# A two-layer RG-LRU / attention block: the attention pieces' time plan shifted, the last gate's vectors moved into the attention, row transposes spread over the first head

## The chip, the cores and the metric

The kernel runs on one core of a Trainium2 chip. The metric is the device time of one execution in microseconds (us). The engines are named as the profile names them: PE (TensorE, matmuls and transposes, with PEld for its weight loads), DVE (VectorE), ACT (ScalarE), POOL (GpSimd) and SP (SyncE, which issues most of the loads here).

## The reference

Two layers run over 512 latent and 256 context tokens of width 2048, all in float32. Layer 0 is a bidirectional RG-LRU, layer 1 a differential attention with 16 heads of two 64-wide parts. Each layer is a norm modulated by a condition vector c, a mixer, and a residual gated by a vector of its own that also comes from c (a product of silu(c) with a 2048-wide matrix, "the gate").

```
for i in range(DEPTH):                       # i = 0 RG-LRU, i = 1 attention
    shift, scale, gate = split(silu(c) @ mod_w[i] + mod_b[i], 3)
    h = rms_norm(x, norm_g[i]) * (1 + scale) + shift     # context too, with c_ctx
    x = x + gate * mixer_i(h, h_ctx)
# attention, per head; q, k normed and rotated; keys are 512 + 256 tokens
    p0, p1 = softmax(q0 @ k0.T), softmax(q1 @ k1.T)
    o = (p0 - lam * p1) @ v
    y = rms_norm(o, subln_g) * (1 - lam_init) * silu(g)   # then y @ w_out
```

## The kernel before

Every float32 product is made of three matmuls on split operands: a weight tile `raw` (128x1024, 512 KB) is cast to its high half `wh` by ACT (line 54), DVE subtracts to get the low half `wl` (line 57), and a step is h times wh, h times wl, low h times wh. Two `raw` buffers take the loads of all weights in turn. PE's order is the order in which the code is written; the other engines and SP's queue are ordered by the compiler's scheduler, and then run strictly in that order.

The program has four stages. The first makes the modulation and the RG-LRU (to about 720 us of the trace). `phase2` is its out-projection: four column blocks n of 512, each 16 steps of six token tiles, with six PSUM accumulators `acc` (lines 530 to 532); `evac` scales by the gate row, adds to x, and sums squares. Beside it runs `mod_stream`, the products of the gates: a 512 KB tile `mw` of the transposed matrix is loaded, and DVE multiplies it by silu(c), broadcast over the partitions, and sums each row (line 108, 128x1024). The gates of layer 0 need both c and c_ctx, so two products a tile; layer 1's gate needs one (32 tiles, the blocks 48 to 63 in two halves). After the last block come the norm of the rows and `norm1`: for each of 16 column tiles kt, the tokens' rows are transposed by PE (`tps`, line 234: four tiles of a latent group or two of the context's) and `h_evac` makes h and its low half, in ACT and DVE. The latent group's 16 turns run before the context tiles' last block is done, the context group's inside head 0.

`phase3` is the attention, `head` by `head`. Head hd's projection has 96 steps, written (b, t, k): four blocks b of weights (two raw tiles each), six token tiles t (t 4 and 5 half as wide), four column tiles k. A step of full width is three matmuls `pj` (lines 676 to 678). Between these steps stand the pieces of the attention of the head before, at due times on a planner's clock that adds 0.68 (0.36 for t 4 and 5) a step and COST a piece; `merged` puts a piece ahead of the first step at which the clock has come to its due time, and what is left behind the last step. These due times are the table PLAN. The pieces:

- k0, k1, q: k and q by channels, transposed.
- s00 to s31: scores of query tile 0 to 3, softmax part 0 or 1, in the one PSUM buffer `sc` (line 754). DVE takes the maximum (756), ACT the exponential with its sum (761), DVE joins the two parts.
- t0a to t3b: transposes of a query tile's probabilities, first four key tiles, then two (`atr`, line 779), into the one PSUM buffer `tr`; ACT casts, DVE subtracts (`athl`).
- v0, v1: their product with v for two query tiles (`o`, lines 790 to 792, 18 matmuls); ACT copies it out.
- o0, o1: transposes of the output back (`otr`, line 802); ACT copies it (804) and squares it.
- f (line 811): DVE's rsqrt of the output's norm (815, 816, and lines 81 to 83) and four products with the gate path (820). y: the transposes of the result (`otr`, line 827).

A prime marks a piece of the head before that one: o1', f' and y' stand early in the next head, since v1 ends the table. At the same place the next head's `qk_norm` runs on DVE: squares' sums (`qv`, 704), rotary products (`pr`, `rt`, 714 to 717) and the scaling (719).

The last turn (hd 16) has no projection; its steps are those of the attention's out-projection (`out_chunks`, two blocks of 64), its own o1, f and y have due times in LAST, and head 15's share of the first block comes at the end.

Of the kernel before, what the change touches and what calls it, by code (L numbers as in the profile page):

```python
# [32 lines left out]
PLAN = ((0.3, "o1'"), (0.5, "f'"), (5.0, "y'"), (17.0, "k0"), (20.5, "k1"), (24.0, "q"), (27.5, "s00"), (31.5, "s01"), (35.5, "s10"),  # L33
        (37.0, "t0a"), (39.2, "t0b"), (39.6, "s11"), (43.6, "s20"), (45.2, "t1a"), (47.4, "t1b"), (47.6, "s21"), (49.6, "v0"),
        (51.8, "s30"), (53.2, "o0"), (54.0, "t2a"), (56.2, "t2b"), (56.4, "s31"), (61.6, "t3a"), (63.8, "t3b"), (66.0, "v1"))
LAST = ((69.5, "o1"), (70.0, "f"), (74.5, "y"))
COST = {"o": 0.2, "f": 0.0, "y": 0.2, "k": 0.3, "q": 0.4, "s": 0.7, "t": 0.3, "v": 2.2}
# [6 lines left out]
class Kern:  # L44
# [114 lines left out]
    def run(self):  # L159
# [379 lines left out]
    def phase2(self):  # L539
# [5 lines left out]
        with tc.tile_pool(name="p2", bufs=1, reuse_waits="tile") as pool:  # L545
            col = pool.tile([128, 64, 2, 2], F32, tag="mcl", name="mcl")
            chunk = lambda h, n, end: [(h, b, 2, end) for b in range(32 + 4 * n, 36 + 4 * n)]
            gates = self.mod_stream(pool, col, chunk(0, 1, 0) + chunk(1, 1, 1) + chunk(1, 2, 0) + chunk(0, 2, 1) + chunk(0, 3, 0)
                                    + chunk(1, 3, 1) + [(h, b, 1, 1 - h) for h in (1, 0) for b in range(48, 64)])
            xt = []  # L550
            for i in range(NTOK):
                t = (pool if i < 4 else pb).tile([128, D], F32, tag=f"x{i}", name=f"x1_{i}")
                xt.append(t)
            ss = [pb.tile([128, GROUPS[g][1], 4], F32, tag=f"ss{g}", name=f"ss{g}") for g in range(2)]
            norm = iter(())
            for n in range(4):
                gt = pool.tile([128, 2, 512], F32, tag="gt", name="gt")
                for grp in ((range(6),) if n < 3 else (range(4), range(4, 6))):
                    acc = {t: self.psum("acc") for t in grp}
# [11 lines left out]
                    for b in range(4):  # L571
                        w = []
                        for u in (2 * b, 2 * b + 1):
                            w.append(self.weights(a["w_out"][n, u], (2, 512)))
                            for _ in range(2 if n > 1 or u % 2 else 1):
                                next(gates, None)
# [8 lines left out]
                        for t in grp:  # L585
                            for k in range(4):
                                self.out_mm(acc, w[k // 2], k % 2, 4 * b + k, (t,))
                            if b:
                                for _ in range(3):
                                    next(norm, None)  # L590
                            if b == 3:
                                evac(t)
                    for _ in norm:
                        pass
                    if n == 3:
# [13 lines left out]
                        norm = self.norm1(g, xt, pb)  # L609
        return norm, lambda: poolb.__exit__(None, None, None)  # L610

    def norm1(self, g, xt, pool):
        for kt in range(KT):
            self.norm_group(1, g, (kt,), xt, pool)
# [44 lines left out]
    def load(self, pool, name, shape, src):  # L659
# [3 lines left out]
        return t  # L663

# [237 lines left out]
    def phase3(self, rest, done):  # L902
# [4 lines left out]
        self.p3a = self.ctx3.enter_context(tc.tile_pool(name="p3c", bufs=1, reuse_waits="tile"))  # L907
        prev = None
        with tc.manual_schedule(engines={nc.tensor.engine}):
            for hd in range(HEADS + 1):  # L910
                prev = self.head(hd, prev, rest, done)
        self.ctx3.close()

    def head(self, hd, prev, rest, done):
# [39 lines left out]
        if last:  # L954
# [130 lines left out]
```

## Time and profile before

| | |
|---|---|
| Time of a run | 2526.28 us median of 3 runs (2524.82 to 2530.53) |
| The profiled execution | 2525.51 us; its span in the trace 2523.7 us |
| Granted TensorE clock, mean | 0.97 of full speed |
| PE busy | 93% of the span |
| DVE busy | 63% |
| ACT busy | 45% |
| DMA, 119 GB/s on average | the queue that carries the weights takes 33.7% of 16 engines' span |

The span is what the trace holds, the time also holds what lies around it. A busy share is an average over the four stages; PE's busy time is that of pipelined matmuls, whose starts are 0.23 us apart while each is shown with 0.39. A granted clock of 1.00 is 2.4 GHz, 0.50 is 1.2 GHz.

### The profile page before, as it was taken

To read this page: it belongs to the slowest core of one execution; us is meant where nothing else is said; L and a number is where in the kernel's file an instruction comes from. 1 tells how busy PE (TensorE), PEld (TensorE's weight loads), DVE (VectorE), ACT (ScalarE), POOL (GpSimd) and SP (SyncE) were. 2 spreads that over 40 slices of the span, in tenths; PEclk is the share of its full clock that TensorE was granted. 3 is DMA by queue.
4 is the path that set the end of the run, shared out by engine and by line. 5 is a ranking of instruction groups with operands and counts; after the bars stand their busy time and mean duration, and the time that the engine had idled before them with its cause. 6 is when DMAs were issued, how large, how long until landed. Compare 5 with 4: busy or idle time off the path is not lost.

```text
span 2523.7 us, 32331 instructions
## 1 busy us (share of the span) xinstructions
PE 2335.4 (93%) x12529; PEld 1943.8 (77%) x12544; DVE 1592.4 (63%) x3029; ACT 1124.0 (45%) x1965; POOL 9.2 (0%) x20
## 2 busy tenths in 40 slices
PE   5989999999999999798999989998999989988999
PEld 4678888888888777587877777777877777777787
DVE  4459999999567756446555564555555564556643
ACT  5367656756862114544433343333433344344421
POOL 0001000000000000000000000000000000000000
PEclk9999999999999999899999999999999999999999
DMA  9915554543247776121121111111121111123242
GB/s 359 377 60 171 179 179 157 172 156 133 73 145 260 254 254 216 52 84 55 52 70 55 55 51 55 55 55 55 59 63 55 55 52 53 55 94 108 80 159 75
DMA packets 93448, 299.43 MB, mean 119 GB/s; under 512 B 11696, under 2 KB 16112, under 8 KB 93296
## 3 DMA queue, kind: packets, MB, share of 16 engines
q1 hardware_dynamic: 88544, 288.41, 33.7%
q10 hardware_dynamic: 4752, 8.98, 0.9%
q8 instruction: 98, 1.61, 0.3%
q14 instruction: 54, 0.44, 0.1%
HBM read 278.52 MB, written 18.83 MB: 118 GB/s over the span
## 4 chain that ended last, share of the span: by engine, by line
PE 54%; DVE 18%; ACT 9%; DMA 7%; issue 4%; SPq 0%; POOL 0%; ACTq 0%; DVEq 0%
PE pj L676 9%; PE pj L677 9%; PE pj L678 9%; DVE wl L57 4%; DMA mw<-mod_t 4%; PE proj L340 4%; PE proj L338 4%; PE proj L342 4%; PE sc L754 3%; ACT wh L54 2%; DVE mw L108 2%; PE acc L532 2%; PE acc L530 2%; PE acc L531 2%; ACT p L761 2%
## 5 line engine op out<-in xcount | busy, mean ns | idle before, releaser
L676 PE MATMUL pj<-wh,h 128*128 128x512 f32 (+1 forms) x1536 | 575.2, 375 | 9.1 <-DVE tmp L564 9.1
L677 PE MATMUL pj<-wl,h 128*128 128x512 f32 (+1 forms) x1536 | 557.0, 363 | 0.1
L678 PE MATMUL pj<-wh,h 128*128 128x512 f32 (+1 forms) x1536 | 555.2, 361 | 0.0
L57 DVE TENSOR_TENSOR wl<-raw,wh 128x1024 fp32r<-128x1024 f32 x264 | 319.0, 1220 | 244.0 <-ACT wh L54 240.8
L54 ACT CAST wh<-raw 128x1024 fp32r<-128x1024 f32 x264 | 271.8, 1050 | 447.3 <-PE pj L678 127.2
L676 PEld LDWEIGHTS pj<-wh,h 128*128 128x128 f32 x1536 | 299.3, 195 | 44.6 <-DVE tmp L564 9.5
L678 PEld LDWEIGHTS pj<-wh,h 128*128 128x128 f32 x1536 | 296.3, 193 | 44.8
L677 PEld LDWEIGHTS pj<-wl,h 128*128 128x128 f32 x1536 | 297.9, 194 | 35.9 <-DVE wl L57 1.0
L338 PE MATMUL proj<-h,wh 128*128 128x256 f32 (+1 forms) x1024 | 270.0, 342 | 7.3 <-DVE h L56 6.2
L340 PE MATMUL proj<-h,wh 128*128 128x512 f32 (+1 forms) x1024 | 276.0, 341 | 0.0
L342 PE MATMUL proj<-h,wl 128*128 128x512 f32 (+1 forms) x1024 | 275.0, 340 | 0.0
L338 PEld LDWEIGHTS proj<-h,wh 128*128 128x128 f32 x1024 | 161.2, 189 | 37.3 <-DVE h L56 7.2
L761 ACT ACTIVATE p<-sc,mx 128x768 f32<-128x768 f32 x128 | 116.2, 908 | 165.1 <-DVE mx L756 164.7
L342 PEld LDWEIGHTS proj<-h,wl 128*128 128x128 f32 x1024 | 162.6, 189 | 25.4 <-issue 2.1
L340 PEld LDWEIGHTS proj<-h,wh 128*128 128x128 f32 x1024 | 162.5, 189 | 25.5 <-issue 2.5
L108 DVE SCALAR_TENSOR_TENSOR mw<-mw,sb 128x1024 f32<-128x1024 f32 x128 | 155.7, 1217 | 39.7 <-DMA mw<-mod_t 32.3
L531 PE MATMUL acc<-wl,h 128*128 128x512 f32 x384 | 154.0, 401 | 12.8 <-DVE wl L57 12.8
L756 DVE TENSOR_REDUCE mx<-sc 128x1 f32<-128x768 f32 x128 | 122.1, 954 | 58.3 <-PE sc L754 57.7
L530 PE MATMUL acc<-wh,h 128*128 128x512 f32 x384 | 153.0, 398 | 1.9 <-ACT wh L54 1.9
L532 PE MATMUL acc<-wh,h 128*128 128x512 f32 x384 | 152.6, 397 | 0.0
L108 DVE SCALAR_TENSOR_TENSOR mj<-mw,sb 128x1024 bf16<-128x1024 f32 x96 | 116.8, 1217 | 36.5 <-DMA mw<-mod_t 18.6
L57 DVE TENSOR_TENSOR athl<-atr,athl 128x512 fp32r<-128x512 f32 (+1 forms) x128 | 71.1, 555 | 91.0 <-ACT athl L54 91.0
(237 smaller groups left out, 3461.2 us busy)
## 6 DMA issues: line engine op xcount, KB each, us to landing
mw<-mod_t SPq DMA_DIRECT2D x128, 512.0 KB, 3.4
raw<-w_att SPq DMA_DIRECT2D x128, 512.0 KB, 3.2
mw<-mod_w SPq DMA_DIRECT2D x64, 512.0 KB, 10.2
raw<-w_in SPq DMA_DIRECT2D x64, 512.0 KB, 3.4
raw<-w_out SPq DMA_DIRECT2D x40, 512.0 KB, 4.5
raw<-w_o SPq DMA_DIRECT2D x32, 512.0 KB, 3.5
sb<-crow SPq DMA_DIRECT2D x7, 1024.0 KB, 6.4
yd<-sg SPq DMA_DIRECT2D x15, 384.0 KB, 3.5
```

The costliest lines, as they stand in the source:

```text
L54: nc.scalar.copy(hi, raw)
L57: return lo_eng.tensor_tensor(lo, raw, hi.bitcast(F32), op=ALU.subtract)
L108: nc.vector.scalar_tensor_tensor(o, w, 1.0, self.sb[:, m, :], op0=ALU.mult, op1=ALU.mult, accum_out=col[:, blk, h, m:m + 1])
L338: nc.tensor.matmul(ps[g][:, :GW[g]], wh, h[g][:, 0, :], start=first, stop=False)
L340: nc.tensor.matmul(ps[g][:, :GW[g]], wh, h[g][:, 1, :], start=False, stop=False)
L342: nc.tensor.matmul(ps[g][:, :GW[g]], wl, h[g][:, 0, :], start=False, stop=last)
L530: nc.tensor.matmul(acc[t], yh, wh, start=(kt == first), stop=False)
L531: nc.tensor.matmul(acc[t], yh, wl, start=False, stop=False)
L532: nc.tensor.matmul(acc[t], yl, wh, start=False, stop=(kt == last))
L676: nc.tensor.matmul(o, h[:, 0, c], wh, start=(kt == 0 and t < 4), stop=False)
L677: nc.tensor.matmul(o, h[:, 0, c], wl, start=False, stop=False)
L678: nc.tensor.matmul(o, h[:, 1, c], wh, start=False, stop=(kt == KT - 1 and t != 4))
```

## The change

The table PLAN gets other due times (all pieces keep their kind; t2b and s31 trade places). In LAST the gate rows of the last out-projection become pieces (g0, g1), and head 15's share of the first block (z) too. The products of layer 1's gate leave `phase2`: a new function `gate1_stream` loads the same 32 tiles of 512 KB into the `raw` buffers, as steps that `fillers` sets at t 3 of the blocks b 0 to 2 in heads 1 to 11, each with two products of half the width. `mod_stream` now goes on by one tile per weight tile. The out-projection's accumulators get a PSUM pool that is closed at its end; the transposes of `norm1` go to the buffers `tr` and `sc` of the attention instead, in head 0: the latent group's first two before the first projections, then one a turn, the context group's one a turn. The tables of the rotation are loaded at the end of head 0.

```diff
-PLAN = ((0.3, "o1'"), (0.5, "f'"), (5.0, "y'"), (17.0, "k0"), (20.5, "k1"), (24.0, "q"), (27.5, "s00"), (31.5, "s01"), (35.5, "s10"),
+PLAN = ((1.0, "o1'"), (1.2, "f'"), (10.6, "y'"), (17.0, "k0"), (20.5, "k1"), (24.0, "q"), (28.2, "s00"), (32.0, "s01"), (36.0, "s10"),
...
-LAST = ((69.5, "o1"), (70.0, "f"), (74.5, "y"))
-COST = {"o": 0.2, "f": 0.0, "y": 0.2, "k": 0.3, "q": 0.4, "s": 0.7, "t": 0.3, "v": 2.2}
+LAST = ((14.6, "g0"), (69.5, "o1"), (70.2, "f"), (71.6, "g1"), (78.5, "y"), (82.0, "z"))
+COST = {"g": 0.4, "z": 2.7, "o": 0.2, "f": 0.0, "y": 0.2, "k": 0.3, "q": 0.4, "s": 0.7, "t": 0.3, "v": 2.2}
...
             gates = self.mod_stream(pool, col, chunk(0, 1, 0) + chunk(1, 1, 1) + chunk(1, 2, 0) + chunk(0, 2, 1) + chunk(0, 3, 0)
-                                    + chunk(1, 3, 1) + [(h, b, 1, 1 - h) for h in (1, 0) for b in range(48, 64)])
+                                    + chunk(1, 3, 1))
...
-                            for _ in range(2 if n > 1 or u % 2 else 1):
-                                next(gates, None)
+                            next(gates, None)
...
     def norm1(self, g, xt, pool):
+
+        nc = self.nc
         for kt in range(KT):
-            self.norm_group(1, g, (kt,), xt, pool)
+            ps = self.ppool.tile([128, 1024], F32, tag="sc", bufs=1, name="tps") if kt % 2 else \
+                self.ppool.tile([128, 512], F32, tag="tr", bufs=1, name="tps")
+            for i in range(GROUPS[g][1]):
+                nc.tensor.transpose(ps[:, 128 * i:128 * i + 128], xt[GROUPS[g][0] + i][:, 128 * kt:128 * kt + 128], self.ident)
+            self.h_evac(1, kt, g, ps, pool, nc.scalar)
             yield
...
+    def gate1_stream(self):
+
+        nc = self.nc
+        col = self.pa.tile([128, 16, 4], F32, tag="gc1", name="gc1")
+        for q in range(4):
+            sb = self.pa.tile([128, 512], F32, tag="sb1", name="sb1")
+            nc.sync.dma_start(sb, self.crow[:, 0, 512 * q:512 * q + 512].partition_broadcast(128))
+            for b in range(0, 16, 2):
+                w = self.raw().rearrange("p (b c) -> p b c", b=2)
+                c = slice(512 * (q % 2), 512 * (q % 2) + 512)
+                nc.sync.dma_start(w, self.a["mod_t"][48 + b:50 + b, q // 2][:, :, c].rearrange("b p c -> p b c"))
+                for i in range(2):
+                    nc.vector.scalar_tensor_tensor(w[:, i, :], w[:, i, :], 1.0, sb, op0=ALU.mult, op1=ALU.mult,
+                                                   accum_out=col[:, b + i, q:q + 1])
+                if q < 3 or b < 14:
+                    yield
...
+            na, nb = norms
+            w = {0: load(0)}
+            next(na)
+            for kt in range(4):
+                next(na)
+                for t in range(4):
+                    self.qkv_mm(w[0], kt, t, ps[t])
+            for _ in range(3):
+                next(na)
+            for lat, b in ((1, 1), (0, 0), (1, 2), (0, 1), (1, 3), (0, 2), (0, 3)):
...
+                        if t == 3 and b < 3:
+                            next(self.gates1, None)
                         for k in range(4):
                             def mm():
```

Three places in the order of the engines follow; a number behind a name tells buffers apart.

DVE, at the end of a head's last steps: the weight halves (`wl`) are done, the next head's `qk_norm` (`qv`, `qri`, `qrw`, `qry`, `pr`, `rt`) is woven into the finish f' (`fv`, `fri`, `frw`, `fry`) of the head before. Before the change:

```order
L704 TENSOR_REDUCE qv<-pr 128x12
L816 SCALAR_TENSOR_TENSOR fv<-so,fv 128x4
L705 TENSOR_SCALAR qv<-qv 128x20
L715 TENSOR_TENSOR pr<-kq,tab 128x768
L81 TENSOR_SCALAR fri<-fv 128x4
L83 TENSOR_SCALAR frw<-fv 128x4
L81 TENSOR_SCALAR qri<-qv 128x20
L83 TENSOR_SCALAR qrw<-qv 128x20
L717 TENSOR_TENSOR pr<-pr,rt 128x512
L82 TENSOR_SCALAR fry<-fri 128x4
L82 TENSOR_SCALAR qry<-qri 128x20
```

And with it:

```order
L717 TENSOR_REDUCE qv<-pr 128x12
L718 TENSOR_SCALAR qv<-qv 128x20
L728 TENSOR_TENSOR pr<-kq,tab 128x768
L81 TENSOR_SCALAR qri<-qv 128x20
L83 TENSOR_SCALAR qrw<-qv 128x20
L829 SCALAR_TENSOR_TENSOR fv<-so,fv 128x4
L730 TENSOR_TENSOR pr<-pr,rt 128x512
L82 TENSOR_SCALAR qry<-qri 128x20
L81 TENSOR_SCALAR fri<-fv 128x4
L83 TENSOR_SCALAR frw<-fv 128x4
L669 SCALAR_TENSOR_TENSOR raw,gc_9382<-raw,sb_12899 128x512 x2
L727 TENSOR_TENSOR rt<-kq,tab 128x4x2x16 x2
```

The row of the finish that needs the squares' sums, line 816 (829 after), moved from the second place of this stretch to the sixth, and a gate step (line 669, two products) stands behind the finish's `frw`, ahead of the rotary products of two tiles.

ACT, from the exponential of s11 to that of s21: `p` is the exponential (line 761, then 774), `athl` the cast of transposed probabilities, `wh` a weight tile's. Before:

```order
L761 ACTIVATE p,l_13759<-sc,mx 128x768
L761 ACTIVATE p,l_13162<-sc,mx 128x768
L54 CAST athl<-atr 128x4x128
L54 CAST wh<-raw 128x1024 x2
L54 CAST athl<-atr 128x2x128
L761 ACTIVATE p,l_13849<-sc,mx 128x768
```

After:

```order
L774 ACTIVATE p,l_13740<-sc,mx 128x768
L54 CAST wh<-raw 128x1024
L774 ACTIVATE p,l_13128<-sc,mx 128x768
L54 CAST athl<-atr 128x4x128
L54 CAST wh<-raw 128x1024
L54 CAST athl<-atr 128x2x128
L698 COPY kq<-pj 128x2x128
L54 CAST v<-pj 128x128
L774 ACTIVATE p,l_13830<-sc,mx 128x768
```

The two weight casts stood together between the two casts of t1a and t1b; one of them now stands ahead of the exponential of s20.

PE, between s30 and s31 (`sc`), with o0 (`otr`), t2a and t2b (`atr`). Before, where s30, a projection step, o0 and the first matmul of the next step stand just ahead of these rows, and the last two rows are s31:

```order
L677 MATMUL pj<-wl,h_8801 128x512
L678 MATMUL pj<-wh,h_8801 128x512
L779 MATMUL atr<-ident,p 128x128 x4
L676 MATMUL pj<-wh,h_8811 128x512
L677 MATMUL pj<-wl,h_8811 128x512
L678 MATMUL pj<-wh,h_8811 128x512
L676 MATMUL pj<-wh,h_8821 128x512
L677 MATMUL pj<-wl,h_8821 128x512
L678 MATMUL pj<-wh,h_8821 128x512
L779 MATMUL atr<-ident,p 128x128 x2
L754 MATMUL sc<-k,q 128x512 x2
L754 MATMUL sc<-k,q 128x256 x2
```

After, from s30, the first two rows, to s31, the last two:

```order
L767 MATMUL sc<-k,q 128x512 x2
L767 MATMUL sc<-k,q 128x256 x2
L815 MATMUL otr<-ident,oT 128x128 x2
L689 MATMUL pj<-wh,h_9017 128x512
L690 MATMUL pj<-wl,h_9017 128x512
L691 MATMUL pj<-wh,h_9017 128x512
L792 MATMUL atr<-ident,p 128x128 x4
L689 MATMUL pj<-wh,h_9047 128x512
L690 MATMUL pj<-wl,h_9047 128x512
L691 MATMUL pj<-wh,h_9047 128x512
L767 MATMUL sc<-k,q 128x512 x2
L767 MATMUL sc<-k,q 128x256 x2
```

Between s30 and s31 stood o0, t2a, t2b and four projection steps; now o0, t2a and two steps. In both, s30 follows v0's last matmul at once.

## Rows read from the trace of the kernel before

**Rows 1.** The page's first part: busy time, share of the span and instructions of each engine.
```profile
PE 2335.4 (93%) x12529; PEld 1943.8 (77%) x12544; DVE 1592.4 (63%) x3029; ACT 1124.0 (45%) x1965; POOL 9.2 (0%) x20
```

**Rows 2.** The view of waits for PE; columns: total us, times, longest us.
```profile
PE otr L827 <- DVE ot L820: 61.6, 15, 4.1
...
PE o L790 <- DVE l L763: 20.7, 15, 1.4
PE acc L531 <- DVE wl L57: 12.8, 7, 2.8
...
PE pj L676 <- DVE tmp L564: 9.1, 1, 9.1
PE atr L779 <- DVE athl L57: 8.0, 16, 0.5
...
PE sc L754 <- ACT p L761: 4.8, 15, 0.3
...
PE grow L133 <- ACT gt L134: 2.5, 1, 2.5
```

**Rows 3.** The timeline of PE around one y'; columns: start us, us, instruction, [idle <-releaser].
```profile
1513.07 1.17 PE L827 MATMUL otr<-ident,ot 128*128 128x128 f32 x4 [4.13 <-DVE ot L820]
1513.90 0.78 PE L676 MATMUL pj<-wh,h 128*128 128x512 f32 x1
...
1519.12 0.39 PE L676 MATMUL pj<-wh,h 128*128 128x512 f32 x1
1519.35 0.39 PE L677 MATMUL pj<-wl,h 128*128 128x512 f32 x1
```

**Rows 4.** Windows; us, busy PE, PEld, DVE, ACT, POOL, then PEclk, DMA share, GB/s.
```profile
1513.80:1519.10 5.30, 5.30 (x14) 4.22 (x14) 1.90 (x3) 0.95 (x2) 0.00 (x0) 0.50 0.14 49
1560.00:1575.00 15.00, 13.06 (x71) 10.17 (x70) 9.55 (x18) 8.08 (x23) 0.00 (x0) 1.00 0.20 71
1508.60:2235.60 727.00, 668.32 (x3584) 555.57 (x3591) 411.79 (x910) 284.94 (x630) 0.00 (x0) 0.96 0.17 56
```

**Rows 5.** The timeline of all engines, from 1500 to 1585 us.
```profile
1504.91 1.22 DVE L57 TENSOR_TENSOR wl<-raw,wh 128x1024 fp32r<-128x1024 f32 x1 [0.52 <-ACT wh L54]
...
1505.51 0.37 ACT L804 COPY ot<-otr 128x256 f32<-128x256 f32 x1
...
1506.91 0.15 DVE L816 SCALAR_TENSOR_TENSOR fv<-so,fv 128x4 f32<-128x4 f32 x1
...
1509.04 0.69 DVE L714 TENSOR_TENSOR rt<-kq,tab 128x128 f32<-128x128 f32 x3
...
1511.71 0.96 DVE L719 TENSOR_TENSOR kq<-pr,qry 128x768 f32<-128x768 f32 x1
1512.58 1.13 DVE L820 SCALAR_TENSOR_TENSOR ot<-ot,fry,g 128x128 f32<-128x128 f32 x4
```

**Rows 6.** The page's fifth part; columns as count | busy, mean ns | idle.
```profile
L54 ACT CAST wh<-raw 128x1024 fp32r<-128x1024 f32 x264 | 271.8, 1050 | 447.3 <-PE pj L678 127.2
...
L761 ACT ACTIVATE p<-sc,mx 128x768 f32<-128x768 f32 x128 | 116.2, 908 | 165.1 <-DVE mx L756 164.7
...
L108 DVE SCALAR_TENSOR_TENSOR mw<-mw,sb 128x1024 f32<-128x1024 f32 x128 | 155.7, 1217 | 39.7 <-DMA mw<-mod_t 32.3
...
L756 DVE TENSOR_REDUCE mx<-sc 128x1 f32<-128x768 f32 x128 | 122.1, 954 | 58.3 <-PE sc L754 57.7
```

**Rows 7.** Windows of the out-projection and of head 0's start; columns as in rows 4.
```profile
852.00:920.00 68.00, 61.47 (x258) 49.29 (x257) 45.62 (x72) 11.30 (x20) 0.00 (x0) 0.95 0.76 256
920.00:1000.00 80.00, 72.63 (x301) 58.80 (x300) 50.91 (x89) 22.50 (x36) 0.00 (x0) 0.91 0.74 244
1015.20:1041.20 26.00, 11.82 (x41) 8.51 (x40) 17.13 (x36) 19.97 (x33) 0.00 (x0) 0.61 0.25 83
```

**Rows 8.** The page's sixth part: loads of two weight kinds, KB, us to landing.
```profile
raw<-w_att SPq DMA_DIRECT2D x128, 512.0 KB, 3.2
...
x<-x SPq DMA_DIRECT2D x16, 256.0 KB, 7.4
```

More of the change, by code (lines that the diff above doesn't have):

```diff
@@ L29 @@
 EPS = 1e-6
-PLAN = ((0.3, "o1'"), (0.5, "f'"), (5.0, "y'"), (17.0, "k0"), (20.5, "k1"), (24.0, "q"), (27.5, "s00"), (31.5, "s01"), (35.5, "s10"),
-        (37.0, "t0a"), (39.2, "t0b"), (39.6, "s11"), (43.6, "s20"), (45.2, "t1a"), (47.4, "t1b"), (47.6, "s21"), (49.6, "v0"),
-        (51.8, "s30"), (53.2, "o0"), (54.0, "t2a"), (56.2, "t2b"), (56.4, "s31"), (61.6, "t3a"), (63.8, "t3b"), (66.0, "v1"))
-LAST = ((69.5, "o1"), (70.0, "f"), (74.5, "y"))
-COST = {"o": 0.2, "f": 0.0, "y": 0.2, "k": 0.3, "q": 0.4, "s": 0.7, "t": 0.3, "v": 2.2}
+PLAN = ((1.0, "o1'"), (1.2, "f'"), (10.6, "y'"), (17.0, "k0"), (20.5, "k1"), (24.0, "q"), (28.2, "s00"), (32.0, "s01"), (36.0, "s10"),
+        (37.6, "t0a"), (39.8, "t0b"), (40.2, "s11"), (44.2, "s20"), (45.8, "t1a"), (48.0, "t1b"), (48.4, "s21"), (51.6, "v0"),
+        (51.8, "s30"), (54.8, "o0"), (55.8, "t2a"), (56.4, "s31"), (58.6, "t2b"), (62.2, "t3a"), (64.4, "t3b"), (66.6, "v1"))
+LAST = ((14.6, "g0"), (69.5, "o1"), (70.2, "f"), (71.6, "g1"), (78.5, "y"), (82.0, "z"))
+COST = {"g": 0.4, "z": 2.7, "o": 0.2, "f": 0.0, "y": 0.2, "k": 0.3, "q": 0.4, "s": 0.7, "t": 0.3, "v": 2.2}
 UL = SEQ + 4 + CTX
@@ L558, in phase2 @@
                 for grp in ((range(6),) if n < 3 else (range(4), range(4, 6))):
-                    acc = {t: self.psum("acc") for t in grp}
+                    acc = {t: self.pp.tile([128, 512], F32, tag="acc", bufs=6, name="acc") for t in grp}
                     c = slice(512 * n, 512 * n + 512)
@@ L993, in head @@
                         self.qkv_mm(w[b], 4 * b + k, t, ps[min(t, 4)])
[L994 to L996 removed]
+                    if lat:
+                        next(na, None)
+                    if lat or 0 < b < 3:
+                        next(nb, None)
             done()
             self.pa = self.ctx3.enter_context(self.tc.tile_pool(name="p3b", bufs=1, reuse_waits="tile", side="right"))
+            tab = self.load(self.pa, "tab", [128, 18, 64], self.tabd)
+            self.cg = {"q": tab[:, 0:4, :], "k": tab[:, 8:14, :]}
+            self.sg = {"q": tab[:, 4:8, :], "k": tab[:, 14:18, :]}
+            self.gates1 = self.gate1_stream()
             begin()
```

76 lines of the change are left out of this document (31 added, 45 removed).

## The prediction

> **What bounds the kernel now.** I read the page's engine table first. TensorE (PE) is busy in 93% of the span [rows 1], so the time is its work plus its waits, and I asked who ends those waits. One row leads: the transposes of a head's finished output, the piece y', stand 61.6 us behind VectorE's (DVE's) line 820, fifteen times, the longest 4.1 us. Far behind come the product with v (20.7), the out-projection's low weight halves (12.8), the first projection of head 0 (9.1, once), the second halves of the probability transposes (8.0), the scores (4.8) and a gate row (2.5) [rows 2].
>
> Then I looked at one y' in order of time. PE waits 4.13 us for it, transposes from 1513.07 to 1513.90, and its next twelve projection matmuls last until 1519.12, after which they start 0.23 us apart again [rows 3]. The reason is the clock: granted 0.50 (1.2 GHz) from 1513.8 to 1519.1, while it is 1.00 in the later stretch of the head that holds a wait for v and one for probabilities [rows 4]. The long idle therefore costs twice. From 1513.07 to 1519.12 are 6.05 us; twelve matmuls at 0.23 and 0.35 us of transposes would be 3.1; so one y' costs 4.13 + 2.95 = **7.1 us**. The same matmul nine heads later is 727.00 us on [rows 4]: a head lasts 80.8 us, its waits included.
>
> **The change, part by part.**
>
> *y' later.* The wait is a chain on ScalarE (ACT) and DVE: the copy of the output starts at 1505.51, its squares follow, line 816 starts at 1506.91, the rsqrt steps are woven into the next head's norm, and line 820 ends at 1512.58 + 1.13 = 1513.71 [rows 5]. The table moves y' from seven projection steps behind o1' to fourteen. Count from the start of v1, whose eighteen matmuls take 2.2 us. At the last of the 96 steps the planner's clock is 66.48, short of v1's new 66.6, so v1 now stands behind the last step. Then come two steps (3 x 0.23 each, 1.4), o1' at 3.6, and fourteen steps (9.6): y' is due at 13.3. The chain: output copy at 3.9 or a little later, line 829 (816 before) 1.40 behind it [rows 5] at 5.3, where DVE arrives at 5.5. The order shows what it does next: 0.7 of rotary sum, 0.3 of small steps, and in heads 2 to 11 the gate step. That waits for its load, which starts when the weight tile before it is read (u = 3.4; the row at 1504.91 is this one before the change [rows 5]) and takes 3.2 us if it lands like a w_att tile, 7.4 if like x's slices in the out-projection [rows 8]. I take the nearer, of the same size and stage: landed at 6.7 to 7.4. Its two half-wide multiplies are priced by one of full width, 1.22 [rows 6], plus reads of the sums: 1.4. From the rotary products to the k scaling 2.7 [rows 5], that scaling 1.0, a rotary product 0.7, four output products 1.13: ready at 14.0 to 14.6, so PE waits about 0.8. Bounds: 0 and, with the slow landing, 4. Heads 12 to 15 have no gate step and are ready 1.7 earlier: no wait.
>
> *The other pieces.* v0 moves 2 us later and t2b behind s31, s01 a little: I count their waits, 1.38, 0.50 and 0.32 (totals over sixteen or fifteen, [rows 2]), as gone, 2.2 a head. New waits come with them:
> - t1b. ACT now casts one weight tile ahead of the exponential of s20, and may do so only after step (b 2, t 5, k 1), 1.3 us behind that score. From the end of s20: cast until 2.35 (1.05 [rows 6]), exponential and its sum until 3.45 (0.91 [rows 6] and 0.2), cast of t1a's transposes until 4.0, DVE's low half until 4.8, while t1b is due at 3.5. Wait: **1.45**. Bounds 0 and 2.
> - s31. s30 follows v0 at once, as before, but o0, a step, t2a and a step (1.9 us) are now all that stands between s30 and s31. Their one PSUM buffer needs maximum (0.95) and exponential (0.91 [rows 6]) and three handovers: 2.4. Wait 0.5; with a gate step ahead of that maximum 1.0. Bounds 0 and 2.
> - s11, behind the gate step in front of s10's maximum: 1.4 of work and no slack but 1.0: 0.45. t2a, t3a, t3b: 0.35 together.
>
> A head with gate steps so gives back 7.1 + 2.2 - (0.8 + 1.45 + 1.0 + 0.45 + 0.35) = 5.2, one without 9.3 - (1.45 + 0.5 + 0.15) = 7.2. Heads 2 to 11: 52. Heads 12 to 15: 28.8. Head 1 has no y', so 2.2 - 3.25 = -1. The last head has one y' (7.1), loses the gate row's 2.5 and the slow clock behind it (about 1.2), and gets the 2.1 of new waits: 8.7.
>
> *Gates out of the out-projection.* 32 loads of 512 KB and 32 multiplies of 1.22 leave this stage; in the attention, where DVE is busy 412 of 727 us and the DMA 17% [rows 4], they come back as 32 loads of the same bytes and 64 half-wide multiplies. The cover there is the slack priced above. Here the DMA is busy 0.76 and 0.74, and from 852 to 1000 PE starts 258 and 301 matmuls in 68 and 80 us; at 0.23 that is 59 and 69, so 19.5 us are lost, clock included [rows 7]. The other 24 gate steps stay, two multiplies each, and now reach to the middle of the third column block. I keep 2.5 for them: gain **17**. Bounds 6 and 19.5.
>
> *Row transposes in head 0.* Before, the first group's transposes run in a bunch, then PE waits 9.1 us for the last eviction [rows 2], since the projection's PSUM banks came free with it. From 1015.2 to 1041.2 there are 27 transposes (0.09 each) and 14 matmuls (3.2), under 6 of 26 us, at clock 0.61 [rows 7]: 20 lost. After, the first two tiles' transposes stand right behind the out-projection, and PE idles while ACT evicts and casts and DVE subtracts, 2.7 us; then twelve matmuls, 2.8 us, cover each tile. If that idle drops the clock, another 2.6. So 5 are lost, gain **15**. Bounds 8 and 19. The tables' load comes later; the first use is behind it, and k0 stands 17 us on.
>
> **Sum.** 52 + 28.8 - 1 + 8.7 + 17 + 15 = 120.5. The profiled execution took 2525.5 us (its span 2523.7), 0.8 below the median of the runs shown: 2525.5 - 120.5 = 2405, and I give **2406** against that median.
>
> **Rivals.**
> - *The chain stays behind y' in the ten heads with gates.* For it: the 7.4 us landing [rows 8], or any 3 us more on DVE, whose queue is strictly in order here. Then each waits over 3 us and the clock falls again: 6.3 x 10 back, **2469**.
> - *The clock still falls.* The change leaves two or three waits of 1 to 1.5 us per head close together. Against it: the stretch 1560 to 1575, with waits of 1.38 and 0.50, ran at 1.00 [rows 4]. If it falls once per head, half of 5.3 us in fifteen heads comes back: 2406 + 40 = **2446**. The Trainium skill ("TensorE: Matmul & The Clock Gate", section "A second HAM failure mode: psum-queue depth-cycling") tells of a kernel whose clock kept swinging because TensorE idled briefly but often between groups of matmuls. By that rule this rival would hold, by the row the forecast; the row speaks for this very pattern, at a lower density than the change makes.
> - *The new waits are twice my size*, since ACT and DVE meet in one place: 4.05 x 11 + 2.1 x 5 = 55 more, **2461**.
> - *Slower.* Each of the 32 gate steps holds DVE's queue until its load lands, and scores, casts and y' behind it wait. At 7.4 us instead of 3.2 a step costs 4.2 and, if the clock follows, 2.5: 32 x 6.7 = 214 against 120, **2619**. It decides from 3.8 us of PE time per step. Against it: DMA share 0.17 in this stage, w_att at 3.2.
> - *Nothing gained*: every y' keeps its wait because the chain moves with o1', and the out-projection its gaps: 2406 + 63 + 5 x 7.1 + 17 = **2521**.
>
> **How the numbers follow.** Forecast 0.58 (its own range 2380 to 2432), chain 0.10, clock 0.09, double waits 0.14, slower 0.05, nothing gained 0.04. All but the last two are faster by more than 0.2%, about what a measurement of this kernel tells from no change (5 us); I give same 0.03 and slower 0.06 with their edges. The low end takes half of the new waits away (-30): 2374. The high end takes the clock and the doubled waits: 2462; left out are the chain case and the last two, 0.19.
>
> **What the profile would show.** Right: the wait of the transposes for line 833 (820 before) under 15 us in all; no stretch at half clock in most heads; nine heads in 670 to 685 us; new rows of some 20 us for the probability transposes behind the low cast and of 10 to 15 for scores behind the exponential; the out-projection's wait for low weight halves under 4 us; no 9 us before head 0's projections. Wrong: PE waiting over 3 us at y', or DVE idle behind the gate tile's DMA by over 2 us a step, or half clock once a head without such a wait.

## The result, and the profile after

The changed kernel takes 2401.11 us (median of 4 runs, 2398.83 to 2402.87); the ratio to the kernel before is 0.9501, with a 95% interval of 0.9485 to 0.9518. The forecast was 2406 us. Its total is close because two of its terms were wrong by about the same amount and in opposite directions, as the stages show.

The page's first part, after: PE is busy in 95% of the span, for [rows 1]'s 93%.

```profile
PE 2287.6 (95%) x12529; PEld 1919.2 (80%) x12544; DVE 1585.9 (66%) x3079; ACT 1126.6 (47%) x1965; POOL 9.3 (0%) x20
```

The waits of PE after (total us, times, longest us), the answer to [rows 2]:

```profile
PE atr L792 <- DVE athl L57: 11.6, 19, 0.7
PE tps L605 <- ACT het L223: 7.4, 9, 0.9
PE acc L520 <- DVE gcol L123: 7.2, 1, 7.2
PE sc L767 <- ACT p L774: 6.5, 15, 0.9
...
PE acc L520 <- DVE tmp L556: 6.0, 4, 2.7
PE pj L689 <- ACT h L54: 4.5, 3, 3.9
...
PE acc L520 <- DVE sg L493: 2.4, 1, 2.4
...
PE otr L840 <- DVE ot L833: 3.1, 3, 1.8
```

The 61.6 us at y' are 3.1 in three waits, and the product with v waits no more. The waits of probability transposes and scores are those that the prediction priced. But the accumulators of the out-projection have new ones, behind DVE's lines 123 and 556, and the row transposes (line 605) wait nine times in head 0.

PE around one y', after (start us, us, instruction; an idle time ahead of it would stand at the row's end), beside [rows 3]:

```profile
1543.75 0.38 PE L815 MATMUL otr<-ident,oT 128*128 128x128 f32 x2
...
1553.52 0.93 PE L840 MATMUL otr<-ident,ot 128*128 128x128 f32 x4
```

No idle time stands in front of y' (line 840), 9.8 us behind o1' (815).

Windows of the kernel before, by stage: the out-projection, from its last matmul to the first of head 0, head 0, head 1, heads 2 to 15, the last turn; a head runs from its first projection matmul to the next one's. Columns as in [rows 4]:

```profile
720.80:1014.20 293.40, 278.66 (x1217) 227.97 (x1216) 200.00 (x328) 88.10 (x137) 0.00 (x0) 0.97 0.70 236
1014.20:1035.10 20.90, 6.72 (x35) 4.63 (x33) 12.93 (x19) 18.69 (x30) 0.00 (x0) 0.66 0.23 76
1035.10:1106.40 71.30, 64.61 (x320) 52.71 (x322) 22.21 (x53) 29.42 (x56) 0.00 (x0) 0.96 0.12 39
1106.40:1179.80 73.40, 71.01 (x394) 59.55 (x393) 45.49 (x86) 30.80 (x64) 0.00 (x0) 1.00 0.22 72
1179.80:2311.50 1131.70, 1040.22 (x5574) 864.67 (x5587) 646.63 (x1424) 448.92 (x991) 0.00 (x0) 0.96 0.18 60
2311.50:2523.60 212.10, 198.00 (x903) 161.36 (x901) 99.05 (x172) 56.78 (x93) 0.00 (x0) 0.97 0.31 104
```

The same stages after:

```profile
723.70:1008.80 285.10, 269.36 (x1185) 220.76 (x1184) 159.23 (x246) 83.41 (x130) 0.00 (x0) 0.98 0.54 179
1008.80:1014.00 5.20, 1.29 (x11) 0.96 (x9) 4.00 (x6) 3.99 (x6) 0.00 (x0) 0.86 0.61 202
1014.00:1096.70 82.70, 73.14 (x376) 57.91 (x377) 29.73 (x60) 47.29 (x84) 0.00 (x0) 0.97 0.16 51
1096.70:1174.20 77.50, 71.07 (x394) 59.90 (x395) 54.41 (x116) 34.25 (x71) 0.00 (x0) 1.00 0.30 100
1174.20:2200.00 1025.80, 1002.43 (x5574) 848.21 (x5587) 673.60 (x1535) 450.98 (x991) 0.00 (x0) 1.00 0.25 81
2200.00:2401.00 201.00, 193.90 (x902) 158.54 (x900) 98.70 (x172) 55.39 (x90) 0.00 (x0) 1.00 0.34 110
```

Read downwards, the gains are 8.3, 15.7, -11.4, -4.1, 105.9 and 11.1 us (and -2.9 ahead of the first row, where the change does nothing; the profiles of the runs below differ there by up to 6). The forecast had 17, 15, nothing of its own for head 0, -1, 80.8 and 8.7. So heads 2 to 15 gave 25 us more than forecast and the last turn 2, and the out-projection, the way to head 0 and heads 0 and 1 together gave 22 less (8.5 for 31). The granted clock of heads 2 to 15 is 1.00 for 0.96, and it is 1.00 in every 4 us of them.

### The profile page after: what moved, and what is told of

The parts are those of the page before. It is cut to its first block, busy times and chain, and to the rows that moved or that the text cites. A ratio compares the mean times of both kernels' runs of the same rounds, so it can differ in the third digit from the quotient of the medians.

```text
span 2401.1 us, 32345 instructions
## 1 busy us (share of the span) xinstructions
PE 2287.6 (95%) x12529; PEld 1919.2 (80%) x12544; DVE 1585.9 (66%) x3079; ACT 1126.6 (47%) x1965; POOL 9.3 (0%) x20
## 4 chain that ended last, share of the span: by engine, by line
PE 64%; DVE 11%; DMA 8%; ACT 6%; issue 3%; POOL 0%; SPq 0%; ACTq 0%; DVEq 0%
PE pj L689 9%; PE pj L691 9%; PE pj L690 9%; PE proj L330 5%; PE proj L328 5%; PE proj L332 5%; PE acc L520 4%; PE acc L522 4%; PE acc L521 4%; PE sc L767 3%; DVE wl L57 2%; DMA raw<-mod_t 2%; DMA mw<-mod_t 2%; ACT p L774 1%; DVE mj L108 1%
## 5 line engine op out<-in xcount | busy, mean ns | idle before, releaser
L689 PE MATMUL pj<-wh,h 128*128 128x512 f32 (+1 forms) x1536 | 566.0, 368 | 5.8 <-ACT h L54 4.5
L691 PE MATMUL pj<-wh,h 128*128 128x512 f32 (+1 forms) x1536 | 547.4, 356 | 0.2 <-DVE h L57 0.2
L690 PE MATMUL pj<-wl,h 128*128 128x512 f32 (+1 forms) x1536 | 546.0, 355 | 0.1
L691 PEld LDWEIGHTS pj<-wh,h 128*128 128x128 f32 x1536 | 289.8, 189 | 45.1 <-DVE h L57 2.2
L689 PEld LDWEIGHTS pj<-wh,h 128*128 128x128 f32 x1536 | 290.2, 189 | 39.8 <-ACT h L54 5.8
L690 PEld LDWEIGHTS pj<-wl,h 128*128 128x128 f32 x1536 | 291.1, 190 | 34.3 <-DVE wl L57 1.0
L520 PE MATMUL acc<-wh,h 128*128 128x512 f32 x384 | 151.6, 395 | 15.7 <-DVE gcol L123 7.2
L767 PE MATMUL sc<-k,q 128*128 128x512 f32 (+1 forms) x512 | 115.3, 347 | 6.5 <-ACT p L774 6.5
L108 DVE SCALAR_TENSOR_TENSOR mw<-mw,sb 128x1024 f32<-128x1024 f32 x96 | 117.4, 1223 | 0.4
```

The source lines that it names most:

```text
L108: nc.vector.scalar_tensor_tensor(o, w, 1.0, self.sb[:, m, :], op0=ALU.mult, op1=ALU.mult, accum_out=col[:, blk, h, m:m + 1])
L520: nc.tensor.matmul(acc[t], yh, wh, start=(kt == first), stop=False)
L689: nc.tensor.matmul(o, h[:, 0, c], wh, start=(kt == 0 and t < 4), stop=False)
L690: nc.tensor.matmul(o, h[:, 0, c], wl, start=False, stop=False)
L691: nc.tensor.matmul(o, h[:, 1, c], wh, start=False, stop=(kt == KT - 1 and t != 4))
```

## The experiments

Ratios are to the kernel before on the same chip. Most intervals are about 0.0015 to each side, so a difference under some 5 us between two kernels isn't told by them; the stages of the traces tell smaller ones, each from one execution. In two profiled executions of the changed kernel the stages above differ by up to 2.1 us.

**The plan alone.**

```diff
-PLAN = ((0.3, "o1'"), (0.5, "f'"), (5.0, "y'"), ...
+PLAN = ((1.0, "o1'"), (1.2, "f'"), (10.6, "y'"), ...
-LAST = ((69.5, "o1"), (70.0, "f"), (74.5, "y"))
+LAST = ((69.5, "o1"), (70.2, "f"), (78.5, "y"))
```

> The kernel before with the new due times alone (PLAN as changed, o1, f and y of LAST too); gates and transposes stay where they were, so heads 2 to 15 hold no gate steps. Theory A, read from the two traces: the whole gain is the plan's, 8.1 us a head as heads 12 to 15 of the changed kernel show, 14 x 8.1 = 113, some 6 in the last head, -2 in head 1: 2409 us. Rival B, the sum of the prediction: 7.2 a head without gate steps, 101, and 6 and -1: 2420 us; the out-projection and the boundary to head 0 then carry 32 us by themselves.

2402.06 us, ratio 0.9527 (0.9508 to 0.9545), by which it would take 2407 us beside the 2526 of the kernel before: the due times give nearly all of the change by themselves. Windows of its out-projection and of heads 2 to 15:

```profile
722.20:1017.30 295.10, 278.52 (x1217) 227.29 (x1216) 200.14 (x328) 88.09 (x137) 0.00 (x0) 0.97 0.70 235
1179.90:2194.30 1014.40, 995.26 (x5574) 847.24 (x5586) 639.05 (x1425) 449.32 (x991) 0.00 (x0) 1.00 0.21 67
```

The out-projection is as long as before; heads 2 to 15 fall from 1131.7 to 1014.4 us, 8.4 a head. Theory A holds (8.1 a head, 2409 us), Rival B (7.2, 2420) does not. The rest is 6.6 us by the ratios. About as much lies in the last turn: it is 208.4 us here (from 2194.3 to the span's end at 2402.7) for the changed kernel's 201, and this run lacks the pieces g0, g1 and z of LAST. So, by these numbers, gates and row transposes together were worth next to nothing.

**o1', f' and y' alone.**

```diff
-PLAN = ((0.3, "o1'"), (0.5, "f'"), (5.0, "y'"), (17.0, "k0"), ...
+PLAN = ((1.0, "o1'"), (1.2, "f'"), (10.6, "y'"), (17.0, "k0"), ...
```

> The kernel before with the due times of o1', f' and y' alone moved. If one wait at y' and the slow clock behind it cost 7.1 us and both go: 15 x 7.1 = 106, 2420 us, granted clock near 1.00 in the heads, a head of 73.7 us. Rival: the clock's fall does not hang on that idle time and stays, so only the wait of 4.1 goes: 2464 us. Rival on the other side: the chain of copy, squares and rsqrt moves along with o1' and the wait stays: 2526 us.

2426.96 us, ratio 0.9622 (0.9606 to 0.9638). Heads 2 to 15:

```profile
1177.60:2217.60 1040.00, 1005.18 (x5574) 845.10 (x5587) 646.68 (x1424) 446.94 (x991) 0.00 (x0) 1.00 0.20 65
```

1040.0 us, 6.55 a head less than before, at clock 1.00: the wait and the slow clock behind it went together, for the 7.1 forecast. Neither rival (2464 and 2526 us) is near. The other pieces are the remaining 25.6 us between this row and the plan's, 1.8 a head.

**The gates back in the out-projection.**

```diff
-                                    + chunk(1, 3, 1))
+                                    + chunk(1, 3, 1) + [(h, b, 1, 1 - h) for h in (1, 0) for b in range(48, 64)])
...
-                            next(gates, None)
+                            for _ in range(2 if n > 1 or u % 2 else 1):
+                                next(gates, None)
...
-                        if t == 3 and b < 3:
-                            next(self.gates1, None)
```

> The changed kernel with the products of layer 1's gate back in the out-projection, at their old pace; plan and transposes as changed. Theory A: the out-projection (285.1 us from its first to its last matmul in the changed kernel) grows by some 5 only, since its waits only moved (27 us of them before, 21 after), and heads 2 to 11 lose the 1.1 us by which they are longer than heads 12 to 15: 2401 + 5 - 11 = 2395 us. Rival B, by the prediction: the out-projection grows by 17, the ten heads lose 2.0 each: 2398 us. The total hardly tells them apart, the length of the out-projection does: 290 or 302 us.

2397.89 us, ratio 0.9506 (0.9491 to 0.952): the same as the changed kernel. The out-projection and heads 2 to 15:

```profile
722.50:1017.80 295.30, 271.99 (x1185) 221.48 (x1184) 198.94 (x327) 83.79 (x130) 0.00 (x0) 0.97 0.69 233
1180.90:2195.50 1014.60, 995.54 (x5574) 848.06 (x5587) 638.80 (x1425) 448.92 (x991) 0.00 (x0) 1.00 0.21 67
```

The out-projection is 10.2 us longer than in the changed kernel, between the two theories, and the heads 11.2 shorter, as theory A had it (11; rival B 20). Neither theory had what stood in the way: this out-projection waits 13.6 us in six waits behind the evictions of line 556.

**The row transposes as before.** This is the kernel before with the new PLAN, LAST and COST and with `gate1_stream`; transposes, accumulators and the tables' load stay as they were:

```diff
-            self.pstag = ("ps", 2)
...
-                    acc = {t: self.pp.tile([128, 512], F32, tag="acc", bufs=6, name="acc") for t in grp}
+                    acc = {t: self.psum("acc") for t in grp}
...
                             for k in range(4):
                                 self.out_mm(acc, w[k // 2], k % 2, 4 * b + k, (t,))
+                            if b:
+                                for _ in range(3):
+                                    next(norm, None)
```

> The changed kernel with the row transposes as before (the first group's in a bunch about the out-projection's end, out of the accumulators' banks). Theory A: the boundary won 15.7 us, but head 0 is 11.4 longer, and the 28 transposes that stood in the last column block cost some 4 there: the part is worth 8 us, 2409 us. Rival B, by the prediction, 15 us: 2416 us.

2388.42 us, ratio 0.9472 (0.9454 to 0.949): not slower but 7 us faster than the changed kernel by the ratios. Both theories had the wrong sign. Its stages, from the out-projection to heads 2 to 15:

```profile
721.50:995.70 274.20, 270.38 (x1217) 223.68 (x1216) 162.46 (x250) 89.86 (x139) 0.00 (x0) 0.99 0.57 188
995.70:1014.70 19.00, 6.38 (x35) 4.52 (x34) 11.63 (x17) 17.03 (x28) 0.00 (x0) 0.62 0.21 71
1014.70:1084.60 69.90, 63.21 (x321) 51.68 (x322) 23.47 (x57) 29.29 (x56) 0.00 (x0) 0.98 0.16 51
1084.60:1158.10 73.50, 70.61 (x396) 59.87 (x395) 50.18 (x104) 32.52 (x67) 0.00 (x0) 1.00 0.31 100
1158.10:2183.00 1024.90, 1001.75 (x5574) 847.63 (x5587) 673.17 (x1535) 450.15 (x991) 0.00 (x0) 1.00 0.25 81
```

Beside the changed kernel's, the out-projection is 10.9 us shorter, though 32 transposes stand in it (eight of the latent group's sixteen turns; in this trace, as in that of the kernel before, the other eight follow behind the stage's last matmul); the way to head 0 is 13.8 longer; head 0 is 12.8 shorter and head 1 4.0: 13.9 in sum. So the gates' leaving did free the out-projection, 293.4 to 274.2, 19.2 us for the 17 forecast; what the changed kernel shows in this stage is that gain less a loss that the transposes' part brought. The loss comes from the two parts together: with the gates in the out-projection, the way from its start to head 2 is 457.7 us with the old transposes (the plan alone, from 722.2 to 1179.9) and 458.4 with the new ones (the gates back, from 722.5 to 1180.9); with the gates out it is 436.6 and 450.5.

**The changed kernel again, and its accumulators in eight banks.** Four kernels ran side by side. The first is unedited:

> The changed kernel itself, unedited, for comparison on the same chip with the three below and, by its ratio to the kernel before, with the kernel that keeps the old transposes: ratio 0.9501 if nothing hangs on the chip, so that the old transposes (0.9472) are worth 7 us; a ratio near 0.953 would make that 15 us, as the two profiled executions have it (2401.1 against 2384.0 us of span).

2397.93 us, ratio 0.9499 (0.9485 to 0.9512): no difference by the chip shows, and the old transposes are worth 7 us by the ratios and 11 (beside this execution) to 13.9 (beside the first) by the stages; only the sign is sure. The out-projection, head 0 and heads 2 to 15 of this execution, with which the runs below are compared (head 1 is 77.6 us):

```profile
720.30:1003.30 283.00, 268.76 (x1186) 220.30 (x1185) 160.07 (x247) 83.78 (x130) 0.00 (x0) 0.99 0.54 180
1007.90:1090.30 82.40, 72.47 (x378) 57.36 (x378) 29.72 (x60) 47.31 (x84) 0.00 (x0) 0.98 0.16 52
1167.90:2194.60 1026.70, 1002.10 (x5588) 848.23 (x5587) 673.45 (x1536) 450.93 (x991) 0.00 (x0) 1.00 0.25 81
```

The second draws the accumulators from all banks:

```diff
-        with tc.tile_pool(name="p2", bufs=1, reuse_waits="tile") as pool, \
-                tc.tile_pool(name="pp2", bufs=1, space=PSUM, reuse_waits="tile") as self.pp:
-            self.pstag = ("ps", 2)
+        with tc.tile_pool(name="p2", bufs=1, reuse_waits="tile") as pool:
...
-                    acc = {t: self.pp.tile([128, 512], F32, tag="acc", bufs=6, name="acc") for t in grp}
+                    acc = {t: self.psum("acc") for t in grp}
```

> The changed kernel with the out-projection's accumulators drawn from all eight PSUM banks, as before the change, in place of six of their own; transposes, gates and plan as changed. Theory C: with six banks a column block can't start until the block before has been scaled and added (its waits stand behind line 556, and at 866 us behind DVE's queue as a whole); with eight it starts in the two spare ones. The waits of 2.5, 2.9, 0.6, 1.5, 1.8 and 7.4 us and the slow clock's 2.4 behind the last go: the out-projection falls from 285.1 to 266 us, the kernel by 19. Rival D: DVE's queue is late because it waits 8.4 us for the reload of silu(c)'s row at the pace of one tile per weight tile; banks don't matter, and the time falls by 3 at most.

2386.8 us, ratio 0.9457 (0.9443 to 0.9472). In the changed kernel, PE at the border of the second and third column block, and DVE there:

```profile
866.33 0.39 PE L522 MATMUL acc<-wh,h 128*128 128x512 f32 x1
873.93 0.77 PE L520 MATMUL acc<-wh,h 128*128 128x512 f32 x1 [7.21 <-DVE gcol L123]
```

```profile
861.57 1.23 DVE L108 SCALAR_TENSOR_TENSOR mj<-mw,sb 128x1024 bf16<-128x1024 f32 x1 [8.44 <-DMA sb<-crow]
...
873.10 0.69 DVE L556 TENSOR_TENSOR tmp<-acc,gt 128x512 f32<-128x512 f32 x1
```

PE has done its block at 866 us and needs a bank for the next; DVE waited 8.44 us for the row `sb`, then worked off gate products, and only at 873.10 comes to the first eviction (line 556), on which the bank hangs. With eight banks the stage is

```profile
722.70:994.10 271.40, 266.87 (x1185) 220.35 (x1184) 159.76 (x247) 84.17 (x130) 0.00 (x0) 0.99 0.56 188
```

11.6 us shorter than in the changed kernel run beside it (283.0), with no wait behind line 556. That is Theory C, but less than its 19: DVE's wait for `sb` is still there (6.39 us, first row), and the weights' low halves come late in its place (second). The longer of these two waits, 2.8 us, ends at 861.77, on a low half that stands in DVE's queue behind the wait for `sb` and the gate products after it; the other, 1.7 us, ends at 842.36, ahead of that wait:

```profile
856.81 1.23 DVE L108 SCALAR_TENSOR_TENSOR mj<-mw,sb 128x1024 bf16<-128x1024 f32 x1 [6.39 <-DMA sb<-crow]
```

```profile
PE acc L522 <- DVE wl L57: 4.5, 2, 2.8
```

The Trainium skill ("Perfetto Trace Analysis", section "Optimizing Tensor Performance") says that independent groups of matmuls should rotate through different PSUM banks, so that one group's eviction overlaps the next one's matmuls. The runs agree: 11.6 us in four column blocks between six banks and eight.

**The reload of silu(c)'s row.**

```diff
-chunk(0, 1, 0) + chunk(1, 1, 1) + chunk(1, 2, 0) + chunk(0, 2, 1) + chunk(0, 3, 0)
-                                    + chunk(1, 3, 1))
+chunk(0, 1, 0) + chunk(1, 1, 1) + chunk(1, 2, 0) + chunk(1, 3, 0) + chunk(0, 2, 1)
+                                    + chunk(0, 3, 1))
```

> The changed kernel with the gate products of the out-projection in another order, so that the row of silu(c) changes halves twice, not three times, and not in the middle of the second column block. Rival D: the wait of 7.4 us and its slow clock, 2.4, go: 10 us less. Theory C: the wait at the end of the second block shrinks to that at the end of the first (2.9, without the clock's fall), the others stay: 5 to 7 us less.

2396.88 us, ratio 0.9491 (0.9476 to 0.9506): no difference that can be told; the out-projection is 281.0 us, 2.0 shorter, no more than two executions differ by. The long wait is gone, but others behind line 556 are as long (7.6 us in three). Theory D falls; C had too much.

**Two buffers for two transposes.**

```diff
-            ps = self.ppool.tile([128, 1024], F32, tag="sc", bufs=1, name="tps") if kt % 2 else \
+            ps = self.ppool.tile([128, 1024], F32, tag="sc", bufs=1, name="tps") if kt % 2 != g else \
```

> The changed kernel with the two PSUM buffers of head 0's transposes exchanged for the context group, so that a turn of the latent and one of the context group no longer share one. The nine waits of 1.07 and 0.64 us between two transposes go, 9 us less. Rival: ACT and DVE, which cast and subtract after every transposes' turn, are the limit in head 0, and the wait moves to the next turn or to the projection: no change over 2 us.

2393.77 us, ratio 0.9479 (0.946 to 0.9498), within its interval of the changed kernel's. Head 0:

```profile
1005.10:1081.10 76.00, 71.49 (x378) 57.98 (x378) 29.00 (x60) 45.47 (x84) 0.00 (x0) 0.97 0.17 56
```

76.0 us for 82.4 in the changed kernel beside it: 6.4 of the nine hoped for, so the shared buffer was most of the wait (7.4 us in nine turns there, 0.4 in one here), and a part moved on to the projection (5.8 us behind the casts of h for 3.9).

**y' a little earlier.**

```diff
-(10.6, "y'")
+(8.4, "y'")
```

> The changed kernel with y' due at 8.4 in place of 10.6: three projection steps, 2.05 us, earlier. The chain on ACT and DVE ends where it did, so PE waits at y' in every head, 2.0 us and in heads with gate steps up to 2.8. Theory: such a wait costs its length and no clock, as the 2.2 us wait of head 2 in the changed kernel left the clock at 1.00: 5 heads x 2.0 + 10 x 2.3 = 33 us more, less a slack of some 0.5 a head: 25 us more, 2423 us. Rival: the clock falls behind it as it did behind 4.1 us, 2.9 more a head: 68 us more.

2428.74 us, ratio 0.963 (0.9614 to 0.9646): 33 us more by the ratios, 25 by the stages from head 2 on. The wait of y', then two of the ten y' rows, in heads 2 and 5, and the windows just behind these two:

```profile
PE otr L840 <- DVE ot L833: 22.6, 10, 3.0
```

```profile
1183.69 1.17 PE L840 MATMUL otr<-ident,ot 128*128 128x128 f32 x4 [2.85 <-DVE ot L833]
```

```profile
1412.38 1.03 PE L840 MATMUL otr<-ident,ot 128*128 128x128 f32 x4 [2.20 <-DVE ot L833]
```

```profile
1183.30:1186.60 3.30, 2.91 (x9) 2.38 (x10) 2.32 (x6) 0.47 (x1) 0.00 (x0) 0.50 0.10 36
1412.40:1415.80 3.40, 3.40 (x16) 2.50 (x18) 1.92 (x5) 0.55 (x2) 0.00 (x0) 1.00 0.11 39
```

Ten waits, 2.3 us on average, in heads 2 to 10 and the last turn; heads 12 to 15, without gate steps, wait nothing even so. Behind 2.85 us the clock was 0.50, behind 2.20 it was 1.00. Four of the ten cost the clock, so the truth lies between the theory's 25 us and the rival's 68. The theory's number is near by luck: five of its fifteen waits did not come (heads 11 to 15), and the clock that it left out fell four times.

**t1b and s31 later.**

```diff
-(48.0, "t1b"), (48.4, "s21"), (51.6, "v0"),
+(48.0, "s21"), (49.4, "t1b"), (51.6, "v0"),
...
-(56.4, "s31"), (58.6, "t2b"),
+(57.1, "s31"), (59.0, "t2b"),
```

> The changed kernel with t1b two steps later, behind s21, and s31 one step later. Theory: the waits of 0.85 (t1b, behind the cast of a weight tile and of t1a) and 0.54 us (s31, behind the exponential of s30) a head are a matter of place alone: 15 x 1.4 = 21 us less, 2377 us. Rival: the pieces behind them (v0 behind t1b, t2b and t3a behind s31) take over the wait: under 8 us less.

2379.04 us, ratio 0.9429 (0.9416 to 0.9442), 17 to 19 us less than the changed kernel. The two waits, 6.5 and 11.6 us in the changed kernel, are now

```profile
PE sc L767 <- ACT p L774: 5.3, 10, 1.9
...
PE atr L792 <- DVE athl L57: 2.4, 7, 0.6
```

and heads 12 to 14 take 70.8 us for 72.3: 1.5 of 1.4. There, place alone made both waits, as the theory says, and the pieces behind don't take them over. In heads with gate steps t1b's is gone too (the row's 2.4 us are t0b's), but s31 still waits, ten times: 1.9 us in head 1, 1.7 in head 8, 0.2 to 0.3 in the others.

**All together, and with later gate steps.** Eight banks, exchanged buffers, the new order of gate products and the later pieces:

> The changed kernel with eight banks for the accumulators, the exchanged buffers of the transposes, the gate products in the order with two reloads, and the later t1b and s31, all together. If these add up: 11 + 6 + 4 (the waits for weight halves at 840 and 858 us, if the late reload makes them) + 20 = 41 us less than the changed kernel: 2357 us, ratio to the kernel before 0.934.

2362.28 us, ratio 0.9364 (0.9347 to 0.938): the fastest version, 34 us under the changed kernel by the ratios, for the 41 that the parts add up to. Its stages, from the out-projection to heads 2 to 15:

```profile
719.10:993.00 273.90, 267.26 (x1186) 220.69 (x1185) 159.73 (x246) 83.17 (x130) 0.00 (x0) 0.99 0.54 182
993.00:997.50 4.50, 1.22 (x10) 0.89 (x8) 3.27 (x5) 3.65 (x6) 0.00 (x0) 1.00 0.58 196
997.50:1073.60 76.10, 71.28 (x377) 57.36 (x378) 29.12 (x60) 45.38 (x85) 0.00 (x0) 0.98 0.17 57
1073.60:1148.70 75.10, 70.81 (x394) 59.98 (x395) 54.40 (x116) 34.31 (x71) 0.00 (x0) 1.00 0.32 104
1148.70:2154.70 1006.00, 998.47 (x5573) 849.63 (x5587) 673.08 (x1535) 451.53 (x991) 0.00 (x0) 1.00 0.25 83
```

Against the changed kernel run again, heads 2 to 15 give 21 us, head 0 6.3, head 1 2.5 and the out-projection 9; the waits for low weight halves (6.6 us) stay, so the new order did nothing for them. The longer, 4.6 us, ends at 860.2, 23 us behind DVE's wait for `sb` (6.28 us, to 836.61): what stands ahead of that low half now is gate products and their own loads, not a reload. With the gate steps in heads 2 to 12:

```diff
-                        if t == 3 and b < 3:
+                        if t == 3 and b < 3 and hd > 1:
```

> As all four together, with the gate steps in heads 2 to 12 in place of 1 to 11. Theory: head 1, 5 us longer than heads 12 to 15 in the changed kernel, is late because the first gate steps and their loads stand in front of its norm of q and k on DVE and hold the weights' buffers: 5 to 6 us less than all four, less 1 that head 12 takes. Rival: it is the tables' load, late in head 0: no change.

2364.85 us, ratio 0.9369 (0.9357 to 0.9382): no change. Head 1, and PE's largest wait about its start:

```profile
1080.00:1154.10 74.10, 73.49 (x394) 62.18 (x395) 48.81 (x102) 32.11 (x69) 0.00 (x0) 0.96 0.22 72
```

```profile
PE pj L688 <- DVE g L700: 3.3, 1, 3.3
```

Its waits for k (3.7 us in all four together) are gone, but PE waits 3.3 us for the gate path of head 0 (line 700) ahead of it. Head 1 keeps 74.1 us of 75.1, at clock 0.96, and head 0 is longer. So the gate steps made these waits, but not the late start: what makes that stays open.

## Why the prediction came out right

The mechanism behind most of the gain was right: the wait at y' and the slow clock behind it, and the waits of the pieces after it. That the total came within 5 us is luck as well: heads 2 to 15 gave 25 us more than summed, and the stages ahead of them 22 less.

**y'** held. The wait and its slow clock, priced at 7.1 us a head, measured 6.55 where nothing else was moved. The rest of it, 0.8 us a head with gate steps, was 3.1 us in three waits (0.3 a head; the longest in head 2, one in the last turn). By the prediction's sum it hung on the load of a gate tile, for which the prediction had 3.2 or 7.4 us. The page's sixth part, after, has its size in KB and its median time to landing:

```profile
raw<-mod_t SPq DMA_DIRECT2D x32, 512.0 KB, 4.1
```

DVE waited 24.9 us for these loads in 25 waits, 0.8 a step and 3.0 at most. The rivals of the chain and of the slower kernel both reckoned with the 7.4. With 4.1 for 3.2 the prediction's sum would have made the wait 1.7 us a head, so some other part of that chain was summed over 1 us too long; which one stays open.

**The other pieces** held in kind and were mis-sized. The waits for t1b and s31 are there, at about half of their price: t1b has 10.4 of its row's 11.6 us, 0.7 a head for 1.45, and s31 6.5, 0.4 a head for 1.0 or 0.5. For t1b the chain was summed too long: in head 12 the low half is done 4.25 us behind s20 (1955.05 to 1959.30) for 4.8, and PE comes for it at 3.6 for 3.5. The 0.5 and 0.45 that a gate step was to add to s31 and s11 did not come: s31 waits 0.36 to 0.47 us in heads with and without one (0.88 in head 10), s11 never. t2a, t3a and t3b hardly show. A head with gate steps gives 7.4 (heads 2 to 11, 80.8 to 73.4) for 5.2, one without 8.1 (heads 12 to 15, 323.9 us to 291.6) for 7.2. In sum heads 2 to 15 gave 105.9 for 80.8: set against the 9.3 that a head was to give back, the new waits cost 1.9 for 4.05 and 1.2 for 2.1.

**Gates out of the out-projection**: 17 forecast, 19.2 measured with the old transposes. The mechanism and the size were right; the changed kernel hides it. In heads 2 to 15 the gate steps cost 10.5 us (1014.4 with the plan alone, 1024.9 with the old transposes) for the 20 priced.

**Row transposes in head 0** is the step that failed: gain 15, bounds 8 and 19. The loss at the boundary fell as worked out, from 20.9 to 5.2 us. But the step counted only the idle time there. It left out that the transposes themselves move into head 0, with a wait in nine of their turns (head 0 is 11.4 us longer, 6.4 of it the shared buffer), and that the accumulators, to make room, kept six banks of eight (11.6 us of the out-projection). Measured as a whole, with the gates out, the part costs 7 us by the runs, 11 to 13.9 by the stages. The change has the six banks in one line (`bufs=6`, which the run with eight banks takes out), and the prediction took no price from that line.

**The last turn** measured 11.1 for 8.7, **head 1** -4.1 for -1. Head 1 takes 73.5 us with the old transposes and 71.8 with the new ones but no gate steps anywhere (1109.1 to 1180.9 us there), so neither alone makes its 77.5. In the range, 2406 less 30 is 2376, not 2374; nothing hangs on it.

So the rivals: the chain behind y' and the clock did not come (no stretch at half clock in heads 2 to 15), the doubled waits were halved instead, and neither slower nor nothing gained was near. The Trainium skill's account of frequent short idles ("TensorE: Matmul & The Clock Gate", section "A second HAM failure mode: psum-queue depth-cycling"), as the prediction read it, would have had the clock fall in the heads; it stayed at 1.00 in all of their 1025.8 us. Of the marks that the prediction set, y' under 15 us, full clock and no 9 us before head 0 came true, and so did the two new rows, at about half of the size named (11.6 us for some 20, 6.5 for 10 to 15); nine heads took 655.9 us (y' from 1480.56 to 2136.47) for the 670 to 685 named, and the wait for low halves is gone, but with evictions in its place.

## What to carry to other kernels

Price a moved piece of work at its new place as well as at its old one: its own engine time, the buffers that it shares there, and what the old place had to give up to let it go. A count of accumulators against banks in a diff is such a price; it shows at block borders, where the eviction stands in an in-order queue behind whatever that engine does else. And where several waits of one head are estimated against the same slack, a run that moves only the due times prices them together: here it shows that they carry nearly all of the gain.

## What was not expected of the hardware

The length of one idle time did not by itself decide the clock. With y' a little earlier, ten waits of 1.7 to 3.0 us stood in like places. The three longest (2.63, 2.85 and 3.00 us) were followed by a stretch at 0.50; so was one of 2.06, while six others, of up to 2.26, were not. What else decides was not tried.

Single executions of one kernel differ by up to 13.6 us here (2386.28 to 2399.83 with two buffers for the transposes), more than those of the kernel before beside them (2521.43 to 2528.06). Which stages that comes from was not looked into.
